# Down-projection of the gated feed-forward layers: a late third output tile at the opening, and four steps of the second group prepared during the first

## The chip, the cores and the metric

The kernel runs on one core of one Trainium2 chip. The metric is the device time of one launch in microseconds (us). Three launches of the kernel before took 1698.48, 1701.52 and 1703.72 us, so the median is 1701.52 us. One more execution was recorded by the hardware profiler; all rows and times of the trace come from it, in us from the first instruction.

## The reference, cut to what matters

Two layers run on 512 latent tokens and 128 context tokens (640 rows), each a token mixer followed by a gated feed-forward block. The change touches only the last product of that block, which is computed once in each of the two layers:

```python
def conv_ffn(h, w_up, conv_w, conv_b, w_down):
    u = h @ w_up                                   # (640, 1024) @ (1024, 5632)
    up = jnp.pad(u, ((0, 0), (1, 1), (0, 0)))
    u = up[:, :-2] * conv_w[0] + up[:, 1:-1] * conv_w[1] + up[:, 2:] * conv_w[2] + conv_b
    a, gt = jnp.split(u, 2, axis=-1)
    return (jax.nn.silu(a) * gt) @ w_down          # (640, 2816) @ (2816, 1024)
...
    xs = xs + g_fs * rmsnorm(fs, norm_ffn_post[l])
```

## The kernel before, in words

**Up-projection.** `ffn` (L1070) makes the 2816 inner columns in 22 pieces of 128 (p = 0 to 21). Each piece is a set of matrix products on PE, evicted by ACT and DVE, then the width-3 convolution in a PSUM tile `t` (ACT L1191, twice DVE L1193), the SiLU (ACT L1199) and the gate product (DVE L1204, `act`), which is stored to DRAM (`act_0` to `act_21`, L1232, on the SP queue). The convolution of the last piece runs after PE's last product.

**Down-projection.** The 640 rows are five output tiles of 128 rows (t = 0 to 4; t = 4 is the context). A tile needs 1024 columns of float32, which is two PSUM banks (`acc`). There are eight banks, so the tiles come in two groups, (0, 1, 2) and (3, 4) (L1337), and each group runs over the 22 steps k of the inner dimension. `load_dn` (L1079) prepares a step: it loads the 128x1024 weight rows (`wr`, 0.5 MB) and the activation columns of the group (`ain`; 384 wide in the first group, 258 in the second), and splits both into a rounded high part and the rest, since the product is made of three passes (high by high, high by low, low by high; `passes`, L166). The high parts `wh` and `ahi` are ACT casts (L155, L1084). The low part `wl` is a subtraction on DVE for even k and on POOL for odd k (L157), `alo` one on DVE (L1086). `go` (L1340) then issues for one tile and one step two halves of three matmuls.

**What sets the order.** `wr`, `wh` and `wl` rotate in four buffers each (pool `wp`), `ahi` and `alo` in four, `ain` in three (pool `dn`). A step can therefore be split only when PE has done all tiles of the step four before it. PE runs its instructions in the order in which the program writes them. The other queues run in the order in which a scheduler placed them, and each is in order, SP's DMA queue too. The first 18 steps go over all tiles of the group; the last four (`tail`) go tile by tile, so that tile 0 is finished first and its bank pair is freed early. While tile 2 does its last four steps, the loop at L1368 prepares steps 0 to 3 of the second group (`NLD` = 4). At the end of a tile, `Finish` does the norm, the residual and, in layer 0, the transposes of the next layer's input (`turns`): square sums on ACT (L327), products on DVE (L344, L346, L356, L365, L371), small scalars on POOL (L329, L336). In layer 0 the transposes of tile 0 run ahead of the last step of tile 2, those of tiles 1 and 2 after steps 3 and 6 of the second group.

**Banks at the opening.** Six of the eight banks belong to the first group. The two banks of tile 2 lie where the convolution tile `t` was, so the first matmul on tile 2 waits for DVE's last read of `t` (L1204).

Of the kernel before, what the change touches and what calls it, by code (L numbers as in the profile page):

```python
# [9 lines left out]
F32 = mybir.dt.float32  # L10
F32R = mybir.dt.float32r
# [7 lines left out]
P = 128  # L19
D = 1024  # L20
# [31 lines left out]
PSN = 4  # L52
PU0 = 6
HALF = (slice(0, 512), slice(512, D))
NLD = 4
KP = (2, 2, 2, 2, 1)
GORDER = ("p s0 t0 va s1 t1 t2".split(), "s0 vb t0 s1 t1 t2".split())

# [33 lines left out]
def hybrid_step(ctx: ExitStack, tc: tile.TileContext, A, O):  # L92
    nc = tc.nc
# [15 lines left out]
    def f32(t):  # L109
        return t.bitcast(F32)  # L110

    def pool(name, bufs=1, side="left", **k):
        return tc.tile_pool(name=name, bufs=bufs, side=side, reuse_waits="tile", **k)

    cst = ctx.enter_context(pool("cst"))
    wp = ctx.enter_context(pool("wp", 4))
# [32 lines left out]

    def wsplit(src, a, b, low=None, own=None, pin=False):  # L150
        q = own or wp
        raw = q.tile([P, a, b], F32, tag="wr", name="wr")
        nc.sync.dma_start(raw, src)
        hi = q.tile([P, a, b], F32R, tag="wh", name="wh")
        i = nc.scalar.copy(hi, raw)  # L155
        lo = q.tile([P, a, b], F32R, tag="wl", name="wl")
        j = (low or nc.vector).tensor_sub(lo, raw, f32(hi))  # L157
        if pin:
            tc.keep_in_program_order(i)
            tc.keep_in_program_order(j)  # L160
        return hi, lo

    def rows(w, r0, nr, c0, ncol):
        return w[r0 * P : (r0 + nr) * P, c0 : c0 + ncol].rearrange("(k p) n -> p k n", p=P)

    def passes(acc, st, w, first, last):  # L166
        for n, (x, y) in enumerate(((st[0], w[0]), (st[0], w[1]), (st[1], w[0]))):
            mm(acc, x, y, start=first and n == 0, stop=last and n == 2)
# [279 lines left out]
    with ExitStack() as s:  # L448
# [57 lines left out]
        def mod_load(i):  # L506
            out = []
            for j in range(4):
                src = rows(A["ada_w"][0], 4 * (j % 2), 4, D - D * (j // 2) + 256 * i, 256)
                how = ADA0[4 * i + j]  # L510
                if how == "r":
                    raw = sp.tile([P, 4, 256], F32, tag="wf", name="wf", bufs=6)
                    nc.sync.dma_start(raw, src)
                    out.append((raw,))
                else:
                    out.append(wsplit(src, 4, 256, nc.gpsimd if how == "p" else None))
            return out
# [41 lines left out]
        def wv_load(i):  # L559
            wv[i] = wsplit(rows(wqkv, 4 * i, 4, 2048, 256), 4, 256, nc.gpsimd)  # L560
# [109 lines left out]
    class Mix:  # L670
# [6 lines left out]
        def weights(self, half, u, low=None):  # L677
            self.ws[half, u] = wsplit(rows(self.w, 2 * u, 2, 512 * half, 512), 2, 512, low, pin=True)
# [35 lines left out]
    with l_na:  # L714
# [268 lines left out]
        for h in range(H):  # L983
# [6 lines left out]
            for i, step in enumerate(order):  # L990
# [15 lines left out]
                if pr and step == "p0":  # L1006
                    sides = []
                    for hh in range(4 * g, 4 * g + 4):
                        qs, kh, kl = qk_of[hh // 2]
                        b = hh % 2  # L1010
# [52 lines left out]
    late = m0.second(fin)  # L1063
# [6 lines left out]
    def ffn(l, hT, hT_close, xold, xnew, nxt, todo, late, late_close, side, back, after=None):  # L1070

        s = ExitStack()
        actd = [dr.tile([P, GAP], F32, name=f"act_{l}_{k}") for k in range(FC)]
        dn = s.enter_context(pool("dn", 4, side))
        cw = cws[l]
        w_up, w_dn = A["ffn_w_up"][l], A["ffn_w_down"][l]
        HB = ((0, 384), (384, GAP))

        def load_dn(k, c0, c1):  # L1079
            w2 = wsplit(rows(w_dn, k, 1, 0, D), 1, D, nc.gpsimd if k % 2 else None)  # L1080
            ain = dn.tile([P, 384], F32, tag="ain", name="ain", bufs=3)
            nc.sync.dma_start(ain[:, 0 : c1 - c0], actd[k][:, c0:c1])
            hi = dn.tile([P, 384], F32R, tag="ahi", name="ahi")
            nc.scalar.copy(hi[:, 0 : c1 - c0], ain[:, 0 : c1 - c0])  # L1084
            lo = dn.tile([P, 384], F32R, tag="alo", name="alo")
            nc.vector.tensor_sub(lo[:, 0 : c1 - c0], ain[:, 0 : c1 - c0], f32(hi[:, 0 : c1 - c0]))  # L1086
            return w2, hi, lo

        lds = deque()
# [7 lines left out]
        with ExitStack() as s2:  # L1097
# [201 lines left out]
            for p in range(PLAIN, FC):  # L1299
                nx = p + 1 if p + 1 < FC else None  # L1300
                for m, q in ((6, p), (5, p), (1, nx), (7, p), (2, nx), (3, p), (4, p)):
                    if q is None:
                        continue
                    evict(m, q, product(m, q))
                    if m == 5:
                        if nx:
                            block_sums(nx)
                        else:
                            lds.append(load_dn(len(lds), *HB[0]))
                    elif m == 7:  # L1310
                        store()
                        if nx:
                            sum_parts(0, nx, nc.gpsimd)
                    elif m == 2:
                        sum_parts(1, nx, nc.gpsimd)
                        if nx + 1 < FC:
                            value(nx + 1, nc.gpsimd)
                    elif m == 3:
                        if not nx:
                            lds.append(load_dn(len(lds), *HB[0]))  # L1320
                        elif nx + 1 < FC:
                            corner(nx + 1)
                    if ada:
                        next(ada, None)
# [8 lines left out]
        xmp = ExitStack()  # L1333
        xmpool = xmp.enter_context(pool("xm", 2, back))
        fin = Finish(l, 5, xold, xnew, nxt, hTn, xmpool, 5, back)
        tail, late = 4, []
        for grp, (c0, c1) in (((0, 1, 2), HB[0]), ((3, 4), HB[1])):  # L1337
            acc = {t: [bk.get("acc") for _ in range(2)] for t in grp}

            def go(t, k, w2, hi, lo, qs=(0, 1)):  # L1340
                c = (t * P if t < 4 else NS + 1) - c0
                for q in qs:
                    passes(acc[t][q], (hi[:, c : c + P], lo[:, c : c + P]),
                           tuple(x[:, 0, 512 * q : 512 * q + 512] for x in w2), k == 0, k == FC - 1)

            for k in range(FC - tail):
                if len(lds) <= k:
                    lds.append(load_dn(k, c0, c1))
                for t in grp:
                    go(t, k, *lds[k])  # L1350
                if nxt and late and k in (3, 6):
                    late.pop(0)()
            for k in range(FC - tail, FC):
                lds.append(load_dn(k, c0, c1))
            prev, lds = lds, deque()
            for t in grp:
                fin.ahead(t)
                if t == 4 and not nxt:
                    for q in range(2):
                        for i in range(tail):  # L1360
                            go(t, FC - tail + i, *prev[FC - tail + i], qs=(q,))
                    fin.end(t, acc[t][0], acc[t][1], fin.stat(acc[t][0]))
                    continue
                for i in range(tail):
                    if nxt and t == 2 and i == tail - 1:
                        late.pop(0)()
                    go(t, FC - tail + i, *prev[FC - tail + i])
                    if t == 2 and i < NLD:  # L1368
                        lds.append(load_dn(i, *HB[1]))
                    if t == 4 and after:  # L1370
                        after(i)
                late.append(fin.end(t, acc[t][0], acc[t][1], fin.stat(acc[t][0])))
# [6 lines left out]
    def gqa_w(c0, u, low=None):  # L1379
        return wsplit(rows(wqkv, 2 * u, 2, c0, 512), 2, 512, low)  # L1380

    wkv = []
    hT, hp2, late, xmp = ffn(
        0, hT, hp1.close, lambda t: xres[0][t], lambda t: xres[1][t], (1, 1, 0, NS),
        ((0, 5), (1, 1), (1, 0), (1, 2), (1, 4), (1, 3)), late, xmp.close, "right", "left",
        lambda u: wkv.append(gqa_w(1024, u)),
    )
# [209 lines left out]
    for hq in range(2):  # L1597
        for n, t in enumerate(((4, 0, 1, 2, 3), (0, 1, 2, 3, 4))[hq]):
# [3 lines left out]
            i = 5 * hq + n  # L1602
# [141 lines left out]
    late = m1.second(fin)  # L1744
# [3 lines left out]
    def y_out(t):  # L1748
        return O["y_sample"][0, t * P : (t + 1) * P, :] if t < 4 else O["y_prompt"][0]

    _, _, _, xmp = ffn(
        1, hT, r_h3.close, lambda t: xres[2][t], y_out, None, ((1, 5),), late, xmp.close, "left", "right"
    )
# [70 lines left out]
```

## Time and profile before

| what | value |
|---|---|
| median of three launches | 1701.52 us (1698.48 to 1703.72) |
| profiled execution, its own time | 1699.22 us |
| its span, first to last instruction | 1697.4 us |
| mean granted TensorE clock | 0.974 |
| layer 0, down-projection (first to last `acc` matmul) | 755.9 to 929.9 us |
| layer 1, down-projection | 1531.5 to 1690.7 us |

A row of the timeline gives the start and the duration of one instruction (or of xN merged ones), the engine, the line, the operation and `out<-in`. Square brackets give the idle time of that engine just before, and what ended it. A matmul's end is modelled, so the pitch from start to start says how fast PE goes.

### The profile page before, as it was taken

The page shows a single profiled execution, that of the slowest core. Times are in us where ns is not written, and L with a number is a line of the kernel's source. Part 1 is how long each engine was busy: PE and PEld are TensorE (multiplying, and loading weights), DVE is VectorE, ACT ScalarE, POOL GpSimd, SP SyncE. Part 2 cuts the span into 40 slices and gives each one's busy share as a digit, 9 for nine tenths or more (in the row PEclk, how much of TensorE's full clock was granted, in tenths as well). Part 3 has the DMA queues.
Part 4 walks back from the last instruction along what each step waited for, and adds up shares of the span by engine and source line. Part 5 has one row for each costly group of instructions (what it writes and reads, how often), then busy time and mean ns, then how long its engine had stood idle before and what let it go on. Part 6 is the DMA issues. An engine that isn't in the chain of part 4 may idle for free.

```text
span 1697.4 us, 26300 instructions
## 1 busy us (share of the span) xinstructions
PE 1589.7 (94%) x9709; PEld 1376.1 (81%) x9709; DVE 1039.7 (61%) x1725; ACT 903.6 (53%) x1721; POOL 751.7 (44%) x651
## 2 busy tenths in 40 slices
PE   6899998999999899989979888999998999998998
PEld 3788897977988788988868666777887999997876
DVE  4444454557875555672375776775696788784264
ACT  5466657655554444553355444664555665663353
POOL 3544545444245354442344345442424555652253
PEclk9999999989999999999989998999999999999999
DMA  9544544116376576347557410001636333336574
GB/s 269 150 112 121 141 127 118 32 63 224 113 235 203 189 218 185 121 153 236 161 187 232 133 38 13 2 1 63 211 112 188 115 120 98 117 117 212 174 238 170
DMA packets 193220, 242.43 MB, mean 143 GB/s; under 512 B 11108, under 2 KB 149572, under 8 KB 193092
## 3 DMA queue, kind: packets, MB, share of 16 engines
q1 hardware_dynamic: 182232, 233.13, 43.7%
q10 hardware_dynamic: 10860, 7.62, 2.3%
q8 instruction: 76, 1.25, 0.3%
q14 instruction: 52, 0.43, 0.1%
HBM read 214.38 MB, written 26.34 MB: 142 GB/s over the span
## 4 chain that ended last, share of the span: by engine, by line
PE 58%; DVE 13%; DMA 8%; POOL 7%; ACT 6%; issue 6%; ACTq 1%; SPq 0%; POOLq 0%; DVEq 0%
PE acc L104 17%; PE ux L104 10%; PE y L104 5%; PE uz L104 4%; PE po L104 3%; PE s L104 3%; DMA wr<-in_ada_w 3%; PE tp L107 3%; PE qk L104 3%; PE uy L104 3%; PE vp L104 3%; DMA wr<-in_na_w_qkv 2%; POOL wl L1117 2%; DVE t L1193 2%; PE ada L104 2%
## 5 line engine op out<-in xcount | busy, mean ns | idle before, releaser
L157 POOL TENSOR_TENSOR wl<-wr,wh 128x1024 fp32r<-128x1024 f32 x80 | 196.3, 2457 | 279.6 <-ACT wh L155 274.9
L1117 POOL TENSOR_TENSOR wl<-wr,wh 128x1024 fp32r<-128x1024 f32 x80 | 194.7, 2451 | 68.7 <-ACT wh L1116 59.3
L104 PE MATMUL ux<-B,wh 128*128 128x322 f32 x832 | 201.9, 313 | 1.9 <-DVE B L210 1.8
L1193 DVE SCALAR_TENSOR_TENSOR t<-C,cw,t 128x644 f32<-128x644 f32 x176 | 156.6, 890 | 55.8 <-ACT t L1191 54.9
L104 PE MATMUL acc<-wh,alo 128*128 128x512 f32 x440 | 175.5, 399 | 10.7 <-DVE alo L1086 10.7
L104 PE MATMUL acc<-wh,ahi 128*128 128x512 f32 x440 | 175.6, 399 | 9.5 <-DVE act L1204 9.5
L155 ACT CAST wh<-wr 128x1024 fp32r<-128x1024 f32 x148 | 153.5, 1047 | 45.0 <-DMA wr<-in_na_w_qkv 17.5
L104 PE MATMUL acc<-wl,ahi 128*128 128x512 f32 x440 | 174.7, 397 | 0.0
L104 PE MATMUL uz<-B,wh 128*128 128x322 f32 x640 | 158.4, 315 | 0.0
L104 PEld LDWEIGHTS ux<-B,wh 128*128 128x128 f32 x832 | 143.6, 189 | 9.6 <-issue 3.3
L1086 DVE TENSOR_TENSOR alo<-ain,ahi 128x384 fp32r<-128x384 f32 (+1 forms) x88 | 55.1, 631 | 141.8 <-ACT ahi L1084 141.8
L104 PE MATMUL ux<-B,wl 128*128 128x322 f32 x416 | 129.2, 311 | 0.0
L1084 ACT CAST ahi<-ain 128x384 fp32r<-128x384 f32 (+1 forms) x88 | 40.5, 462 | 166.3 <-PE acc L104 139.8
L104 PE MATMUL qk<-hT,wh 128*128 128x384 f32 (+1 forms) x512 | 126.6, 320 | 0.4 <-DVE qs L799 0.4
L104 PEld LDWEIGHTS uz<-B,wh 128*128 128x128 f32 x640 | 111.6, 190 | 6.6 <-issue 3.7
L1117 POOL TENSOR_TENSOR vl<-wr,vh 128x1024 fp32r<-128x1024 f32 x38 | 96.5, 2540 | 34.2 <-ACT vh L1116 34.2
L104 PEld LDWEIGHTS acc<-wh,alo 128*128 128x128 f32 x440 | 84.4, 192 | 30.4 <-DVE alo L1086 11.9
L1116 ACT CAST wh<-wr 128x1024 fp32r<-128x1024 f32 x88 | 89.5, 1049 | 35.0 <-DVE wr L1140 33.6
L104 PEld LDWEIGHTS acc<-wh,ahi 128*128 128x128 f32 x440 | 84.6, 192 | 28.4 <-issue 10.2
L1191 ACT ACTIVATE t<-C,cw 128x644 f32<-128x644 f32 x88 | 78.7, 894 | 50.7 <-DVE C L1221 47.4
L157 DVE TENSOR_TENSOR wl<-wr,wh 128x1024 fp32r<-128x1024 f32 x68 | 91.1, 1353 | 21.5 <-ACT wh L155 21.0
L104 PE MATMUL uz<-B,wl 128*128 128x322 f32 x320 | 100.0, 313 | 0.5 <-POOL wl L1117 0.4
(264 smaller groups left out, 4193.8 us busy)
## 6 DMA issues: line engine op xcount, KB each, us to landing
wr<-in_ada_w SPq DMA_DIRECT2D x88, 512.0 KB
wr<-in_ffn_w_up SPq DMA_DIRECT2D x88, 512.0 KB
wr<-in_ffn_w_down SPq DMA_DIRECT2D x88, 512.0 KB
act<-act SPq DMA_DIRECT2D x44, 321.0 KB
wr<-in_na_w_qkv SPq DMA_DIRECT2D x24, 512.0 KB
mod<-modrow SPq DMA_DIRECT2D x20, 512.0 KB
ain<-act SPq DMA_DIRECT2D x44, 192.0 KB
xres<-xo SPq DMA_DIRECT2D x15, 512.0 KB
```

What stands on the lines that cost most here:

```text
L104: pe(nc.tensor.matmul(*a, **k))
L107: pe(nc.tensor.transpose(*a, **k))
L155: i = nc.scalar.copy(hi, raw)
L157: j = (low or nc.vector).tensor_sub(lo, raw, f32(hi))
L1084: nc.scalar.copy(hi[:, 0 : c1 - c0], ain[:, 0 : c1 - c0])
L1086: nc.vector.tensor_sub(lo[:, 0 : c1 - c0], ain[:, 0 : c1 - c0], f32(hi[:, 0 : c1 - c0]))
L1116: nc.scalar.copy(hl[0], src)
L1117: low.tensor_sub(hl[1], src, f32(hl[0]))
L1191: nc.scalar.activation(t, taps(0), AF.Identity, bias=cw[:, 3, n : n + 1], scale=cw[:, 1, n : n + 1])
L1193: nc.vector.scalar_tensor_tensor(t, taps(d), cw[:, w, n : n + 1], t, op0=ALU.mult, op1=ALU.add)
```

## The change: what it does

- **Opening.** In the first group, steps 0, 1 and 2 (`DLEAD` = 3) are done for tiles 0 and 1 only. After step 2, tile 2 does steps 0, 1 and 2 in one go, and from step 3 on all three tiles run together as before.
- **Preloads.** After steps 8, 10, 12 and 14 of the first group (`DPRE`), `load_dn` is called for steps 0 to 3 of the second group, into a pool of their own (`dn2`, four buffers each of `wh`, `wl`, `ahi`, `alo`, three of `ain`). Their raw weights still come through the four `wr` buffers of `wp`.
- **Tail.** During the last four steps of tile 2 the loop now prepares steps 4 to 7 of the second group instead of 0 to 3, in the buffers of `wp` and `dn`.

The number of matmuls, casts, subtractions and loads is the same. The last line of the file and many others move by one to three lines; L104 of before is L105 after, L155 is L156, L1084 is L1086.

```diff
-NLD = 4
+DLEAD = 3
+DPRE = (8, 10, 12, 14)
...
     def wsplit(src, a, b, low=None, own=None, pin=False):
         q = own or wp
-        raw = q.tile([P, a, b], F32, tag="wr", name="wr")
+        raw = wp.tile([P, a, b], F32, tag="wr", name="wr")
         nc.sync.dma_start(raw, src)
         hi = q.tile([P, a, b], F32R, tag="wh", name="wh")
...
-        def load_dn(k, c0, c1):
-            w2 = wsplit(rows(w_dn, k, 1, 0, D), 1, D, nc.gpsimd if k % 2 else None)
-            ain = dn.tile([P, 384], F32, tag="ain", name="ain", bufs=3)
+        def load_dn(k, c0, c1, own=None):
+            w2 = wsplit(rows(w_dn, k, 1, 0, D), 1, D, nc.gpsimd if k % 2 else None, own)
+            p = own or dn
+            ain = p.tile([P, 384], F32, tag="ain", name="ain", bufs=3)
             nc.sync.dma_start(ain[:, 0 : c1 - c0], actd[k][:, c0:c1])
-            hi = dn.tile([P, 384], F32R, tag="ahi", name="ahi")
+            hi = p.tile([P, 384], F32R, tag="ahi", name="ahi")
             nc.scalar.copy(hi[:, 0 : c1 - c0], ain[:, 0 : c1 - c0])
-            lo = dn.tile([P, 384], F32R, tag="alo", name="alo")
+            lo = p.tile([P, 384], F32R, tag="alo", name="alo")
...
-        tail, late = 4, []
+        tail, late, pre = 4, [], deque()
+        dn2 = s.enter_context(pool("dn2", 4, side))
...
                 for t in grp:
-                    go(t, k, *lds[k])
+                    if t != 2 or k >= DLEAD:
+                        go(t, k, *lds[k])
+                if t == 2 and k == DLEAD - 1:
+                    for j in range(DLEAD):
+                        go(2, j, *lds[j])
+                if t == 2 and k in DPRE:
+                    pre.append(load_dn(len(pre), *HB[1], dn2))
...
-            prev, lds = lds, deque()
+            prev, lds, pre = lds, pre, deque()
...
-                    if t == 2 and i < NLD:
-                        lds.append(load_dn(i, *HB[1]))
+                    if t == 2:
+                        lds.append(load_dn(len(lds), *HB[1]))
```

The instruction order shows three places, all in layer 0.

PE at the opening of the down-projection, before: `wh_8191` and `wh_8236` are the weights of steps 0 and 1, `acc_8294` is the second half of tile 1, `acc_8295` and `acc_8296` are tile 2, `acc_8291` is the first half of tile 0.

```order
L104 MATMUL acc_8294<-wh_8191,ahi_8197 128x512
L104 MATMUL acc_8294<-wl_8193,ahi_8197 128x512
L104 MATMUL acc_8294<-wh_8191,alo_8199 128x512
L104 MATMUL acc_8295<-wh_8191,ahi_8197 128x512
L104 MATMUL acc_8295<-wl_8193,ahi_8197 128x512
L104 MATMUL acc_8295<-wh_8191,alo_8199 128x512
L104 MATMUL acc_8296<-wh_8191,ahi_8197 128x512
L104 MATMUL acc_8296<-wl_8193,ahi_8197 128x512
L104 MATMUL acc_8296<-wh_8191,alo_8199 128x512
L104 MATMUL acc_8291<-wh_8236,ahi_8242 128x512
```

The same engine after the change, 24 matmuls further on: `wh_8326` is step 2, `acc_8297` the second half of tile 1, `acc_8298` and `acc_8299` are tile 2.

```order
L105 MATMUL acc_8297<-wh_8326,ahi_8332 128x512
L105 MATMUL acc_8297<-wl_8328,ahi_8332 128x512
L105 MATMUL acc_8297<-wh_8326,alo_8334 128x512
L105 MATMUL acc_8298<-wh_8191,ahi_8197 128x512
L105 MATMUL acc_8298<-wl_8193,ahi_8197 128x512
L105 MATMUL acc_8298<-wh_8191,alo_8199 128x512
L105 MATMUL acc_8299<-wh_8191,ahi_8197 128x512
L105 MATMUL acc_8299<-wl_8193,ahi_8197 128x512
L105 MATMUL acc_8299<-wh_8191,alo_8199 128x512
L105 MATMUL acc_8298<-wh_8236,ahi_8242 128x512
```

Tile 2's first matmul stood behind 12 `acc` matmuls and now stands behind 36.

ACT from the last convolution of the up-projection on, before (the first cast is that of step 4, since steps 0 to 3 are split during the up-projection):

```order
L1191 ACTIVATE t<-C,cw_83 128x2x322
L1084 CAST ahi<-ain 128x384
L155 CAST wh<-wr 128x1024
L1084 CAST ahi<-ain 128x384
L155 CAST wh<-wr 128x1024
L1084 CAST ahi<-ain 128x384
L155 CAST wh<-wr 128x1024
L1084 CAST ahi<-ain 128x384
L155 CAST wh<-wr 128x1024
```

The same place after the change, where the 258 wide casts and the second of the merged weight casts are those of the second group:

```order
L1193 ACTIVATE t<-C,cw_83 128x2x322
L1086 CAST ahi<-ain 128x258 x2
L1086 CAST ahi<-ain 128x384
L156 CAST wh<-wr 128x1024
L1086 CAST ahi<-ain 128x384
L156 CAST wh<-wr 128x1024
L1086 CAST ahi<-ain 128x384
L156 CAST wh<-wr 128x1024
L1086 CAST ahi<-ain 128x258 x2
L1086 CAST ahi<-ain 128x384
L156 CAST wh<-wr 128x1024 x2
```

The scheduler put the four activation casts of the preloads well ahead of step 8, two of them in front of the cast of step 4.

SP at the end of the first group, before (`act_21` with 384 columns is the last activation load of the first group, 258 columns are the second group's):

```order
L1082 DMA ain<-act_21_4825 128x384
L153 DMA wr<-in_ffn_w_down 128x1024
L1082 DMA ain<-act_0_4804 128x258
L153 DMA wr<-in_ffn_w_down 128x1024
L1082 DMA ain<-act_1_4805 128x258
```

The same place after the change:

```order
L1084 DMA ain<-act_21_4825 128x384
L154 DMA wr<-in_ffn_w_down 128x1024
L1084 DMA ain<-act_4_4808 128x258
L154 DMA wr<-in_ffn_w_down 128x1024
L1084 DMA ain<-act_5_4809 128x258
```

The loads that stood here for steps 0 to 3 are now those for steps 4 to 7.

## The prediction

> **What bounds the kernel now.** I began with the page's busy times and its chain of work that ended last.
>
> ```profile
> PE 1589.7 (94%) x9709; PEld 1376.1 (81%) x9709; DVE 1039.7 (61%) x1725; ACT 903.6 (53%) x1721; POOL 751.7 (44%) x651
> PE 58%; DVE 13%; DMA 8%; POOL 7%; ACT 6%; issue 6%; ACTq 1%; SPq 0%; POOLq 0%; DVEq 0%
> ```
>
> PE is busy 94% of the span, and 58% of the chain is PE. The change neither adds nor removes a matmul, so it can only move the gaps in PE's row. I therefore read PE's timeline through both down-projections and looked for starts that lie further apart than the usual pitch. The opening of layer 0:
>
> ```profile
> 755.93 0.40 PE L104 MATMUL acc<-wh,ahi 128*128 128x512 f32 x1
> ...
> 758.47 0.39 PE L104 MATMUL acc<-wh,alo 128*128 128x512 f32 x1
> 763.57 0.76 PE L104 MATMUL acc<-wh,ahi 128*128 128x512 f32 x1 [4.71 <-DVE act L1204]
> ...
> 769.18 0.40 PE L104 MATMUL acc<-wl,ahi 128*128 128x512 f32 x1
> ```
>
> The first two rows are the first and the twelfth matmul, on tiles 0 and 1: the pitch is 2.54 / 11 = 0.231 us. A step of two tiles (12 matmuls) is then 2.77 us, of three tiles 4.16 us. Tile 2 waits for its banks until DVE's last read, and starts at 763.57. The gap costs 5.10 less a pitch, **4.87**. What follows is slow: 13 matmuls take 769.18 - 763.57 = 5.61 instead of 13 x 0.231 = 3.00, another **2.61**.
>
> The change of groups in layer 0, on PE:
>
> ```profile
> 854.42 0.39 PE L104 MATMUL acc<-wl,ahi 128*128 128x512 f32 x1
> 861.15 0.80 PE L104 MATMUL acc<-wh,alo 128*128 128x512 f32 x1 [6.34 <-DVE alo L1086]
> ...
> 864.70 0.40 PE L104 MATMUL acc<-wl,ahi 128*128 128x512 f32 x1
> ...
> 874.60 0.40 PE L104 MATMUL acc<-wl,ahi 128*128 128x512 f32 x1
> 878.19 0.70 PE L104 MATMUL acc<-wh,alo 128*128 128x512 f32 x1 [3.19 <-DVE alo L1086]
> ...
> 881.67 0.42 PE L104 MATMUL acc<-wl,ahi 128*128 128x512 f32 x1
> ```
>
> The second group's first and fifth steps wait for `alo` (854.42 is the eighth matmul of the first step). The gaps cost 6.73 - 0.23 = **6.50** and 3.59 - 0.23 = **3.36**, the eight slow matmuls after each 3.55 - 1.85 = **1.70** and 3.48 - 1.85 = **1.63**. Why `alo` is late, in the rows of ACT, DVE and POOL:
>
> ```profile
> 849.19 0.41 ACT L1084 CAST ahi<-ain 128x258 fp32r<-128x258 f32 x1 [0.38 <-PE acc L104]
> 865.37 1.05 ACT L155 CAST wh<-wr 128x1024 fp32r<-128x1024 f32 x1 [7.21 <-PE acc L104]
> 847.83 1.41 DVE L371 SCALAR_TENSOR_TENSOR xm<-xm,ro,mod 128x512 f32<-128x512 f32 x2 [0.80 <-POOL ro L336]
> 855.18 5.57 DVE L371 SCALAR_TENSOR_TENSOR xm<-xm,ro,mod 128x512 f32<-128x512 f32 x2 [1.08 <-POOL ro L336]
> 860.68 0.75 DVE L1086 TENSOR_TENSOR alo<-ain,ahi 128x258 fp32r<-128x258 f32 x2
> 874.30 3.50 DVE L371 SCALAR_TENSOR_TENSOR xm<-xm,ro,mod 128x512 f32<-128x512 f32 x2 [3.45 <-POOL ro L336]
> 855.12 5.09 POOL L157 TENSOR_TENSOR wl<-wr,wh 128x1024 fp32r<-128x1024 f32 x2
> ```
>
> The first cast of the second group starts only at 849.19, when PE frees a buffer in tile 2's tail, less than 4 us before PE wants the step. Its `alo` then stands on DVE behind the residual of tile 1 (L371), which takes 5.57 beside two POOL subtractions, against 1.41 when POOL is quiet. The fifth step's cast waits 7.21 for PE to finish the first, and its `alo` stands behind tile 2's L371, which ends at 877.8.
>
> Layer 1, PE again, the opening and the change of groups:
>
> ```profile
> 1531.48 0.39 PE L104 MATMUL acc<-wh,ahi 128*128 128x512 f32 x1
> ...
> 1533.99 0.39 PE L104 MATMUL acc<-wh,alo 128*128 128x512 f32 x1
> 1539.13 0.77 PE L104 MATMUL acc<-wh,ahi 128*128 128x512 f32 x1 [4.75 <-DVE act L1204]
> ...
> 1543.95 0.39 PE L104 MATMUL acc<-wh,alo 128*128 128x512 f32 x1
> ...
> 1628.76 0.39 PE L104 MATMUL acc<-wl,ahi 128*128 128x512 f32 x1
> 1630.28 0.50 PE L104 MATMUL acc<-wh,alo 128*128 128x512 f32 x1 [1.13 <-DVE alo L1086]
> ```
>
> The opening costs 5.14 - 0.23 = **4.91** and, over 11 slow matmuls, 4.82 - 2.54 = **2.28** behind it; the change of groups 1.52 - 0.23 = **1.29**.
>
> **The change part by part.** *Opening.* Tiles 0 and 1 now fill 36 matmuls, 36 x 0.231 = 8.32 us, so PE reaches tile 2 at 755.93 + 8.32 = 764.25, and the banks are free at 763.57: 0.68 to spare. In layer 1 it is 1531.48 + 8.32 = 1539.80 against 1539.13, 0.67 to spare. Steps 1 to 3 are split during the up-projection, so nothing else is asked for earlier than it is there. All four terms go: 4.87 + 2.61 + 4.91 + 2.28 = 14.67. If PE comes earlier than the banks by some tenths, the wait is these tenths; bounds 0 to 0.7, I take 0.
>
> What is late next is step 4: its buffers come free when tile 2 has done step 0, at 764.25 + 6 x 0.231 = 765.6. What a split takes is in the page's groups (mean ns after the busy time), the rest in the rows above: `ahi` 0.41 and `alo` 0.38 us in the narrow form, somewhat more in the wide one.
>
> ```profile
> L157 POOL TENSOR_TENSOR wl<-wr,wh 128x1024 fp32r<-128x1024 f32 x80 | 196.3, 2457 | 279.6 <-ACT wh L155 274.9
> L155 ACT CAST wh<-wr 128x1024 fp32r<-128x1024 f32 x148 | 153.5, 1047 | 45.0 <-DMA wr<-in_na_w_qkv 17.5
> L157 DVE TENSOR_TENSOR wl<-wr,wh 128x1024 fp32r<-128x1024 f32 x68 | 91.1, 1353 | 21.5 <-ACT wh L155 21.0
> ```
>
> Two casts (about 1.6) and the low part (1.35 on DVE, 2.46 on POOL for odd steps) make step 4 ready by 768.6; PE wants it after 18 more matmuls of tile 2 and 18 of step 3, at 772.6. Step 5 is ready about 771.5 and wanted at 776.7. So nothing is charged here.
>
> *Preloads.* Each is a load of 0.5 MB and one of 129 KB, two casts on ACT, `alo` on DVE, and `wl` on DVE or POOL. The first group from 764 on, and a denser stretch (PE, PEld, DVE, ACT, POOL busy, clock, DMA share, GB/s):
>
> ```profile
> 764.00:842.00 78.00, 78.00 (x335) 64.27 (x335) 21.07 (x27) 26.50 (x37) 21.50 (x9) 0.97 0.64 203
> 1625.00:1650.00 25.00, 23.87 (x104) 19.16 (x103) 19.54 (x22) 14.98 (x25) 15.66 (x9) 1.00 0.83 272
> ```
>
> In 78 us DVE is busy 21.1, ACT 26.5, POOL 21.5; the preloads add 2 x 1.35 + 4 x 0.38 = 4.2, 4 x (1.05 + 0.41) = 5.8 and 2 x 2.46 = 4.9. DMA moves 203 GB/s, and 2.6 MB more in a slightly shorter time make about 250, under the 272 of the second row. A split can be done three steps (12 us) ahead of its use, so this work lies beside PE and costs nothing. The cover is gone only if loads are later than that (rival 3). On SP two of the preloads' activation loads are queued ahead of the store of `act_21`. They wait for PE's last up-projection product, which ends about when `acc` begins (755.93), while the store waits for DVE until 763.5; they hold nothing back. On ACT two casts of preloads stand ahead of step 4's, whose buffers come free later than these.
>
> *Change of groups.* Steps 0 to 3 are ready long before. Steps 4 to 7 now get the times that steps 0 to 3 had: `alo` of steps 4 and 5 at 860.68 to 861.4. PE runs on from 854.42 without a gap and wants step 4 after 41 more matmuls and eight transposes (a row of eight takes 0.8 here), at 854.42 + 9.47 + 0.8 = 864.7, 3 us later. The transposes of tile 1, wanted at 863.9, need the L371 that ends at 860.7. Tile 2's are wanted three steps later, at 864.7 + 8.3 = 873.0. Their L371 ends at 877.8 in this trace, but its part of the residual stood behind the cast at 865.37 and a POOL subtraction that are both gone from there; I reckon it done about 871. So layer 0's terms go, 6.50 + 1.70 + 3.36 + 1.63 = 13.19, and layer 1's 1.29. For the new meeting points I charge 1 us, bounds 0 and the 3.4 of the old second gap; nearest to nothing, because both margins are positive.
>
> *Clock.* The four long gaps are each followed by matmuls twice as far apart, the gap of 1.13 by none: 2.61 + 1.70 + 1.63 + 2.28 = 8.22 of the sum is this aftermath. The Trainium skill, "TensorE: Matmul & The Clock Gate", section "What's actually happening", says that the PE clock halves after an idle window of about 3.4 us and comes back after about 3.4 us of work. The traces agree in kind. By the page alone four recoveries would cost an estimated 4 x 1.7 = 6.8 us and the sum would be 1.4 smaller.
>
> *Sum.* 14.67 + 13.19 + 1.29 = 29.15, less 1, is 28.15 us. Layer 0's 20.67 must survive to the end: its successor's loads wait for buffers that PE frees, so they move along. The profiled execution took 1699.22 (span 1697.4 and 1.8 around it), 2.3 below the median of the launches, inside their spread. The sum made against it is 1671.1, against the median 1673.4; I take **1672**.
>
> **The rivals.** *1. A new wait in the second group.* DVE and POOL hold each other up: 5.57 against 1.41 above. If tile 1's or 2's residual, or step 4's `alo`, slips by one or two POOL subtractions (2.46 each), PE waits at a transpose or a step. For it: the margins there are 2 to 3 us. Against it: step 4's rows inherit times that have been measured. Price: about the old second gap with its slow tail, 5.0, at most twice that: 1677 to 1682. The Trainium skill, "SBUF — State Buffer", section "Who interferes with whom", says that a DVE instruction with two SBUF inputs and a GpSimd one that reads SBUF exclude each other for the whole instruction. The rows of L371 agree.
>
> *2. Only one half works.* If tile 2 still came too early, or waited for something else, 14.5 of gain would be left, 1701.5 - 14.5 = 1687; if the preloads gave nothing, 14.67 would be left, also 1687. Against it: both openings end on the same DVE line, and by its rows the new order has 0.67 to spare.
>
> *3. Slower: the four `wr` buffers starve the first group.* In steps 8 to 15, twelve loads instead of eight pass through four buffers in 33.3 us, so one turn of a buffer may take 11.1 us. A turn is the landing, 1.05 on ACT and up to 2.46 on POOL, so the pace holds while a load lands within 7.6 us. One landing can be bounded in layer 1, from SP's and ACT's rows:
>
> ```profile
> 1634.28 0.33 SPq L153 DMA_DIRECT2D wr<-in_ffn_w_down  x1
> 1638.71 1.05 ACT L155 CAST wh<-wr 128x1024 fp32r<-128x1024 f32 x1 [1.70 <-DMA wr<-in_ffn_w_down]
> ```
>
> About 4.4 us, at a DMA share of 0.83, so it should hold. Each us over 7.6 delays the stretch by three turns, and the first 12 us are covered. The kernel becomes slower than before from a landing of about 16 us on ((16.3 - 7.6) x 3 - 12 = 14.1 per layer). At 20 us it loses 25.2 per layer, 50.4 - 28.2 = 22 net: 1724.
>
> *4. The change does nothing.* If other engines, not PE, set the pace after each gap, the gaps would reopen later: 1701. PE's 94% speaks against it.
>
> **How the numbers follow.** Forecast 1672, between 1667 and 1676, chance 0.70; rival 1, 1677 to 1682, 0.17; rival 2, 1687, 0.07; rival 4, 0.03; rival 3, 0.03. The range 1665 to 1682 takes in the forecast with its unknown charge, the 2.6 by which launches spread, and rival 1: 0.87, of which some may fall outside. A measurement of this kernel tells about 0.3%, 5.1 us, from no change: faster 0.94, within 0.3% 0.03, slower 0.03.
>
> **What would show it.** In PE's timeline of the changed kernel: the first matmul on tile 2 right behind 36 others in both layers; no gap over 0.7 us and no doubled pitch in the openings; no wait for `alo` at the change of groups; layer 0's down-projection (755.9 to 929.9 now) about 20 us shorter and layer 1's (1531.5 to 1690.7) about 8.5. ACT's `wh` cast should not wait for a `wr` load in the first group. I am wrong if PE waits at a transpose in the second group (rival 1), if the opening's gap stays (rival 2), or if the first group's steps grow beyond 4.2 us around steps 8 to 15 (rival 3).

## The result and the profile after

The kernel after takes 1670.82 us (median of four launches, 1668.97 to 1672.89), the one before 1700.0 (four launches, 1695.11 to 1703.72). The ratio is 0.983, with a 95% interval of 0.9807 to 0.9853: 29.2 us gone. The forecast was 1672, between 1667 and 1676. The profiled execution took 1669.39, 29.83 less than that of before; its span went from 1697.4 to 1667.6.

From the page after, the engines' busy times and shares:

```profile
PE 1579.6 (95%) x9709; PEld 1371.5 (82%) x9709; DVE 1057.2 (63%) x1725; ACT 902.5 (54%) x1721; POOL 751.7 (45%) x651
```

PE's count is the same. Its busy time fell by 10.1 us, all of it in the `acc` matmuls (525.8 to 515.7), since fewer of them run at half rate; the rest of the 29.8 is waiting that is gone.

The opening of layer 0 after, PE's timeline (the first `acc` matmul, then the last on tile 1 and the first on tile 2), and of layer 1:

```profile
755.35 0.40 PE L105 MATMUL acc<-wh,ahi 128*128 128x512 f32 x1
...
763.33 0.39 PE L105 MATMUL acc<-wh,alo 128*128 128x512 f32 x1
763.55 0.39 PE L105 MATMUL acc<-wh,ahi 128*128 128x512 f32 x1
...
1510.35 0.40 PE L105 MATMUL acc<-wh,ahi 128*128 128x512 f32 x1
...
1518.29 0.39 PE L105 MATMUL acc<-wh,alo 128*128 128x512 f32 x1
1518.52 0.39 PE L105 MATMUL acc<-wh,ahi 128*128 128x512 f32 x1
```

Tile 2 follows 36 matmuls (8.20 and 8.17 us) at the usual pitch. DVE's last reads of `t` in the same trace:

```profile
762.02 0.83 DVE L1206 TENSOR_TENSOR act<-t,sl 128x644 f32<-128x644 f32 x1
...
1517.05 0.83 DVE L1206 TENSOR_TENSOR act<-t,sl 128x644 f32<-128x644 f32 x1
```

They end at 762.85 and 1517.88, which is 0.70 and 0.64 before PE starts on tile 2. In the kernel before, PE started 0.15 after the same read had ended (763.42 and 763.57), so the real spare time is about 0.55 and 0.49.

The change of groups in layer 0, PE's timeline around the transposes of tile 1 and tile 2, which stand where the second group's steps 4 and 7 begin:

```profile
856.90 0.39 PE L105 MATMUL acc<-wh,alo 128*128 128x512 f32 x1
857.13 1.04 PE L108 MATMUL tr<-ident,xm 128*128 128x128 f32 x8
857.92 0.48 PE L105 MATMUL acc<-wh,ahi 128*128 128x512 f32 x1
...
866.34 1.03 PE L108 MATMUL tr<-ident,xm 128*128 128x128 f32 x8
867.13 0.48 PE L105 MATMUL acc<-wh,ahi 128*128 128x512 f32 x1
```

DVE there:

```profile
847.04 5.70 DVE L372 SCALAR_TENSOR_TENSOR xm<-xm,ro,mod 128x512 f32<-128x512 f32 x2 [1.08 <-POOL ro L337]
852.66 0.75 DVE L1088 TENSOR_TENSOR alo<-ain,ahi 128x258 fp32r<-128x258 f32 x2
...
861.22 1.42 DVE L372 SCALAR_TENSOR_TENSOR xm<-xm,ro,mod 128x512 f32<-128x512 f32 x2 [1.08 <-POOL ro L337]
```

Tile 1's residual is as slow as before (5.70 against 5.57), and `alo` of steps 4 and 5 still stands behind it, until 853.4. But PE wants it at 858.5 only, because it has steps 0 to 3 to do. The residual is no shorter; PE no longer waits for it. Tile 2's residual is now quick (1.42 against 3.50) and ends at 862.6, 3.7 ahead of its transposes.

Over both down-projections PE has no gap over 0.7 us and no doubled pitch. From the first to the last `acc` matmul, layer 0 takes 153.17 us (173.98 before), layer 1 150.48 (159.17): 20.81 + 8.69 = **29.50**, all of the gain but 0.3.

### The profile page after: what moved, and what is told of

Read it like the earlier page. It is cut to its first block, busy times and chain, and to the rows that moved or that the text cites. A ratio compares the mean times of both kernels' runs of the same rounds, so it can differ in the third digit from the quotient of the medians.

```text
span 1667.6 us, 26282 instructions
## 1 busy us (share of the span) xinstructions
PE 1579.6 (95%) x9709; PEld 1371.5 (82%) x9709; DVE 1057.2 (63%) x1725; ACT 902.5 (54%) x1721; POOL 751.7 (45%) x651
## 4 chain that ended last, share of the span: by engine, by line
PE 47%; DVE 10%; POOL 6%; DMA 4%; issue 4%; ACT 3%; ACTq 0%; SPq 0%; POOLq 0%; DVEq 0%
PE acc L105 18%; PE ux L105 9%; PE uz L105 5%; PE y L105 3%; PE uy L105 3%; POOL wl L1119 3%; DMA wr<-in_ada_w 3%; PE po L105 2%; PE s L105 2%; PE tp L108 2%; DVE t L1195 1%; DVE al L1119 1%; POOL vl L1119 1%; PE ada L105 1%; POOL rh L1437 1%
## 5 line engine op out<-in xcount | busy, mean ns | idle before, releaser
L105 PE MATMUL ux<-B,wh 128*128 128x322 f32 x832 | 201.9, 314 | 1.8 <-DVE B L211 1.7
L156 ACT CAST wh<-wr 128x1024 fp32r<-128x1024 f32 x148 | 153.3, 1047 | 59.6 <-DMA wr<-in_ffn_w_down 28.2
L105 PE MATMUL acc<-wh,alo 128*128 128x512 f32 x440 | 172.0, 391 | 0.0
L105 PE MATMUL acc<-wh,ahi 128*128 128x512 f32 x440 | 171.9, 391 | 0.0
L105 PE MATMUL acc<-wl,ahi 128*128 128x512 f32 x440 | 171.8, 390 | 0.0
L105 PE MATMUL uz<-B,wh 128*128 128x322 f32 x640 | 158.5, 316 | 0.0
L105 PEld LDWEIGHTS ux<-B,wh 128*128 128x128 f32 x832 | 143.8, 189 | 9.5 <-issue 3.7
L1088 DVE TENSOR_TENSOR alo<-ain,ahi 128x384 fp32r<-128x384 f32 (+1 forms) x88 | 74.4, 856 | 89.7 <-ACT ahi L1086 89.3
L105 PE MATMUL ux<-B,wl 128*128 128x322 f32 x416 | 129.3, 311 | 0.0
L105 PE MATMUL qk<-hT,wh 128*128 128x384 f32 (+1 forms) x512 | 126.1, 319 | 0.5 <-DVE qs L800 0.4
L105 PEld LDWEIGHTS uz<-B,wh 128*128 128x128 f32 x640 | 111.9, 190 | 6.6 <-issue 4.1
L1086 ACT CAST ahi<-ain 128x384 fp32r<-128x384 f32 (+1 forms) x88 | 40.1, 460 | 118.9 <-PE acc L105 88.7
L105 PE MATMUL uz<-B,wl 128*128 128x322 f32 x320 | 100.2, 313 | 0.6 <-POOL wl L1119 0.4
L105 PEld LDWEIGHTS acc<-wl,ahi 128*128 128x128 f32 x440 | 82.6, 188 | 17.9
L105 PEld LDWEIGHTS acc<-wh,alo 128*128 128x128 f32 x440 | 82.6, 188 | 17.8
```

The costliest lines, as they stand in the source:

```text
L105: pe(nc.tensor.matmul(*a, **k))
```

## The experiments

All ratios are taken against runs of the kernel before on the same chip (medians 1699.29 for e1 to e4, 1698.88 for e5 and e6, 1696.26 for e7 and e8). A stretch is the time from the first to the last `acc` matmul of a layer in the profiled execution. "Slow" counts the pitches over 0.39 us behind a gap (0.43 is the full half rate; a single one of 0.34 right behind a gap is only the restart).

| kernel | median us | ratio, 95% interval | stretch L0, L1 | PE gaps over 0.6 in L0 (slow after) | in L1 |
|---|---|---|---|---|---|
| before | 1700.0 | | 173.98, 159.17 | 4.87 (12), 6.50 (8), 3.36 (8) | 4.91 (11), 1.29 (0) |
| after | 1670.82 | 0.9807 to 0.9853 | 153.17, 150.48 | none | none |
| e1_opening_only | 1681.46 | 0.9875 to 0.9923 | 165.41, 151.89 | 6.51 (12), 2.96 (0) | 1.29 (0) |
| e2_preloads_only | 1683.53 | 0.9884 to 0.9944 | 160.81, 158.28 | 4.87 (13) | 4.93 (13) |
| e3_lead2 | 1671.25 | 0.9815 to 0.9876 | 155.47, 152.54 | 2.16 (0) | 1.94 (0) |
| e4_two_preloads | 1674.82 | 0.9807 to 0.9881 | 155.90, 150.52 | 1.08 (0), 1.40 (0) | none |
| e5_dense | 1670.45 | 0.9818 to 0.9851 | 153.18, 150.49 | none | none |
| e6_before_dve_low | 1697.54 | 0.9972 to 1.0004 | 170.73, 156.98 | 4.89 (12), 2.35 (7), 4.28 (7) | 4.93 (7) |
| e7_burst | 1671.41 | 0.9819 to 0.9876 | 153.18, 150.52 | none | none |
| e8_lead4 | 1671.28 | 0.9829 to 0.9883 | 153.18, 151.22 | none | 0.61 (0) |

The launches of one kernel spread over some 4 to 14 us; the stretches without gaps agree within 0.05. The spread comes from outside: the first `acc` matmul of layer 0 falls between 753.6 and 760.4 in these traces, and from the end of L0's stretch to the start of L1's pass 597.1 to 602.2. So e3 to e5, e7 and e8 are judged by the stretches; by their times none can be told from the kernel after.

**The opening alone.** The four preloads are taken out, so that the tail prepares steps 0 to 3 of the second group, as before:

```diff
-DPRE = (8, 10, 12, 14)
+DPRE = ()
...
-        dn2 = s.enter_context(pool("dn2", 4, side))
...
-                    pre.append(load_dn(len(pre), *HB[1], dn2))
+                    pre.append(None)
```

> Only the opening is kept (tile 2 joins after three steps); steps 0 to 3 of the second group are prepared in tile 2's tail as before. Theory (each half removes its own gaps and the doubled pitch behind them, and they add): the openings' 14.67 us go, the change of groups keeps its 14.5, so about 1700.0 - 14.7 = 1685 us; layer 0's down-projection 174.0 - 7.5 = 166.5 us with gaps of about 6.5 and 3.4 at its change of groups, layer 1's 159.2 - 7.2 = 152.0. Rival (the halves depend on each other, because the time won at the opening is only lent until the next wait on the split of the second group): the gaps at the change of groups grow by what the opening won, 1695 us or more.

It took 1681.46 against 1699.29. PE at the change of groups of layer 0:

```profile
844.69 0.39 PE L105 MATMUL acc<-wl,ahi 128*128 128x512 f32 x1
851.43 0.80 PE L105 MATMUL acc<-wh,alo 128*128 128x512 f32 x1 [6.35 <-DVE alo L1088]
...
865.79 0.40 PE L105 MATMUL acc<-wl,ahi 128*128 128x512 f32 x1
868.98 0.50 PE L105 MATMUL acc<-wh,alo 128*128 128x512 f32 x1 [2.79 <-DVE alo L1088]
```

The openings' gaps are gone and stay gone, the two gaps behind `alo` are where they were (6.74 - 0.23 = 6.51 and 3.19 - 0.23 = 2.96). The stretches are 8.57 and 7.28 shorter, against 7.48 and 7.19 for the openings' terms; the 1.1 more in layer 0 comes from the second gap and the clock: the second gap is 0.40 shorter and has no slow matmul behind it instead of eight (1.63), the first has twelve instead of eight (0.8 more).

**The preloads alone.**

```diff
-DLEAD = 3
+DLEAD = 0
```

> Only the preloads are kept; tile 2 runs in every step from the first, as before. Theory: both openings keep gaps of 4.9 us and the doubled pitch behind them, the change of groups loses its gaps, so about 1700.0 - 14.5 = 1685.5 us; layer 0's down-projection 174.0 - 13.2 = 160.8 us, layer 1's 159.2 - 1.3 = 157.9. Rival (steps 4 to 7 meet the same jam as steps 0 to 3 did once the first group is not shortened): a gap of 2 to 6 us appears in layer 0's second group, 1690 us or more.

It took 1683.53 against 1699.29. The openings, layers 0 and 1:

```profile
757.41 0.39 PE L105 MATMUL acc<-wh,alo 128*128 128x512 f32 x1
762.51 0.77 PE L105 MATMUL acc<-wh,ahi 128*128 128x512 f32 x1 [4.71 <-DVE act L1206]
...
1518.33 0.39 PE L105 MATMUL acc<-wh,alo 128*128 128x512 f32 x1
1523.49 0.77 PE L105 MATMUL acc<-wh,ahi 128*128 128x512 f32 x1 [4.77 <-DVE act L1206]
```

Both are as before, and no gap is left at the changes of groups. The stretches are 13.17 and 0.89 shorter, against 13.19 and 1.29 for these terms (layer 1's opening had two slow matmuls more in this trace, 2.68 against 2.28). The two halves make 15.85 + 14.06 = 29.9, both together 29.50: they add, and neither needs the other. The medians (17.8 and 15.8 us below their kernel before) are too spread to test this, with intervals of 13.1 to 21.2 and 9.5 to 19.7.

**Two steps of lead instead of three.**

```diff
-DLEAD = 3
+DLEAD = 2
```

> Tile 2 joins after two steps instead of three, the preloads stay. PE then reaches tile 2 after 24 matmuls, 5.54 us, while the banks come 7.64 us after the first matmul: a gap of 2.1 us in each layer. Theory A (the doubled pitch comes only after a gap above a threshold that lies between the 1.1 us gap that had none and the 3.2 us gap that had it): 4.2 us lost in all or up to 3.4 more if 2.1 is above the threshold in both layers; without it 1675 us and no pitch of 0.43 behind the gap. Theory B (the slow stretch grows with the gap, about half of it): 4.2 + 2 = 6.3 us lost, 1677 us, with a few matmuls at 0.43. The Trainium skill, TensorE: Matmul & The Clock Gate, section What's actually happening, puts the threshold at an idle window of about 3.4 us; by it there is no slow pitch here.

PE at tile 2's start, layers 0 and 1:

```profile
760.66 0.39 PE L105 MATMUL acc<-wh,alo 128*128 128x512 f32 x1
763.05 0.47 PE L105 MATMUL acc<-wh,ahi 128*128 128x512 f32 x1 [2.01 <-DVE act L1206]
...
1513.19 0.39 PE L105 MATMUL acc<-wh,alo 128*128 128x512 f32 x1
1515.36 0.47 PE L105 MATMUL acc<-wh,ahi 128*128 128x512 f32 x1 [1.78 <-DVE act L1206]
```

The wait for DVE is back, at 2.16 and 1.94: what 24 matmuls (5.5 us) leave of the 7.65 and 7.39 until the banks are free. The stretches are 2.30 and 2.06 longer than after, 4.4 together, and the doubled pitch stays away. That is theory A with 2.1 below its threshold, and not theory B; but e6 below has the doubled pitch behind a gap of 2.35 and e1 none behind 2.96, so no threshold on the gap alone holds. Three steps is the smallest lead that covers the banks. The time, 1671.25 (1669.11 to 1678.03), does not resolve the 4.4.

**Four steps of lead.**

```diff
-DLEAD = 3
+DLEAD = 4
```

> DLEAD = 4: tile 2 comes in after 48 matmuls instead of 36, nothing else. Theory (the opening only needs to be longer than the 7.64 us until the banks are free; 36 matmuls are 8.32 us): nothing is left to win, PE has no gap over 0.7 us at tile 2's start, and the two stretches stay at 153.2 and 150.5 us. The buffers of step 4 come free 12 x 0.231 = 2.8 us later than with 3 steps, at about 768.4 us, and step 4 is ready about 3 us later, 771.4, against 772.6 when PE wants it; odd steps are 1.1 us later. So a gap up to 1 us may stand at step 4 or 5. Time 1669 to 1674. Rival (buffers, not banks, set the pace at the opening: the split of step 4 and 5 is late once tile 2 starts later): a gap of 2 us or more at step 4 or 5 in both layers, with slow matmuls, 1675 to 1682.

No gap in layer 0, and one of 0.61 in layer 1, at step 13 and not at step 4 or 5, where it was looked for. PE, then POOL and ACT just before:

```profile
1559.63 0.39 PE L105 MATMUL acc<-wh,ahi 128*128 128x512 f32 x1
1560.47 0.50 PE L105 MATMUL acc<-wl,ahi 128*128 128x512 f32 x1 [0.45 <-POOL wl L158]
...
1555.33 7.75 POOL L158 TENSOR_TENSOR wl<-wr,wh 128x1024 fp32r<-128x1024 f32 x3 [5.58 <-ACT wh L156]
...
1554.20 2.00 ACT L156 CAST wh<-wr 128x1024 fp32r<-128x1024 f32 x2 [5.24 <-DMA wr<-in_ffn_w_down]
```

PE waits there for the second of three low parts that stand in a row on POOL (it ends at 1560.41), and they stand in a row after ACT had waited 5.24 for a weight load and then cast several weights close together. So there is nothing left to win beyond three steps; the rival's gaps of 2 us at steps 4 and 5 did not come, but with four steps the cover of the loads was used up at this one place. The cover can be read from the rows as the time from the end of a step's `alo` on DVE to the first matmul that uses it, for steps 5 to 17 of the first group. It is 11.6 us for every step of the kernel before, at least 4.9 (layer 0) and 4.6 (layer 1) after the change, and at least 5.4 and 1.75 here. Why the load came that late was not followed.

**Two preloads instead of four.**

```diff
-DPRE = (8, 10, 12, 14)
+DPRE = (8, 10)
```

> Only steps 0 and 1 of the second group are preloaded, during steps 8 and 10; the tail prepares steps 2 to 5. Theory (the preloads buy PE time until the split of the tail is through the jam of tile 1's residual, 8.7 us after the first transposes): PE wants step 2 about 6.3 us after the start of these transposes and waits some 2.4 us in layer 0, perhaps 0 to 3 more at step 6, and not at all in layer 1: 1673 to 1677 us. Rival (each preload is worth a fourth of the gaps): half of 14.5 comes back, 1678 us, with a gap in layer 1 too.

PE in layer 0's second group:

```profile
856.87 0.40 PE L105 MATMUL acc<-wl,ahi 128*128 128x512 f32 x1
858.18 0.51 PE L105 MATMUL acc<-wh,alo 128*128 128x512 f32 x1 [0.92 <-DVE alo L1088]
...
869.81 0.40 PE L105 MATMUL acc<-wh,ahi 128*128 128x512 f32 x1
871.44 0.50 PE L105 MATMUL acc<-wl,ahi 128*128 128x512 f32 x1 [1.23 <-DVE wl L158]
```

Two steps give PE two times 12 matmuls less cover, and two small gaps come back, 1.08 at step 2 and 1.40 at step 6; layer 1 needs no more than two. The places are those expected, and the first gap is less than half of the 2.4 that was reckoned. So the third and fourth preload are worth 2.7 us by the stretches.

**The preloads denser, and in one burst.** First behind four steps in a row, then all four behind step 14, which asks most of the four `wr` buffers:

```diff
-DPRE = (8, 10, 12, 14)
+DPRE = (8, 9, 10, 11)
```

> The four preloads come after steps 8, 9, 10 and 11 instead of every second step, so that eight weight loads instead of six pass through the four raw buffers within four steps. Theory (loads and splits are three steps ahead, and a load lands in about 4.4 us): no gap on PE, the same time as the changed kernel, 1671 us within 2. Rival (the four raw buffers starve the first group: a turn may take only 16.6 / 2 = 8.3 us here, of which 3.5 are splits, so that loads must land in 4.8 us): ACT's weight casts wait for loads in steps 10 to 15 and PE waits some us before step 16, 1675 us or more.

```diff
-DPRE = (8, 10, 12, 14)
+DPRE = (14,)
...
-                    pre.append(load_dn(len(pre), *HB[1], dn2))
+                    for j in range(4):
+                        pre.append(load_dn(j, *HB[1], dn2))
```

> All four preloads are written behind step 14 of the first group, in a row, instead of behind steps 8, 10, 12 and 14; the same work. The question is how far the first group's loads are ahead of their use. After the change ACT's weight cast waited for loads 13.3 us in all in layer 0's first group, though PE never waited. Theory (the cover is about three steps, 12 us, and four more loads take one turn of the four wr buffers, about 4.4 + 1.05 + 2.46 = 8 us): ACT waits longer in one place, PE does not wait or under 1 us per layer, and the time is that of the kernel after, 1668 to 1674. Rival (the cover is only about one load, and ACT's waits of up to 4.6 us were already its end): PE waits 3 us or more for alo or wl of steps 15 to 17 in each layer, with slow matmuls behind it, and the time is 1676 to 1686.

Both have the stretches of the kernel after, within 0.04. ACT's waits for weight loads in 755 to 850 us (us in total, times, longest us), of the kernel after:

```profile
ACT wh L156 <- DMA wr<-in_ffn_w_down: 13.3, 5, 4.6
```

of the dense one:

```profile
ACT wh L156 <- DMA wr<-in_ffn_w_down: 10.8, 5, 3.4
```

and of the burst:

```profile
ACT wh L156 <- DMA wr<-in_ffn_w_down: 8.7, 6, 2.9
```

ACT does wait for loads, which it never did in this part before, but PE does not wait in any of the three. The burst was to make the longest wait longer, and made it shorter, 2.9 against 4.6 (3.6 against 2.6 for an activation load), so its expectation was right on PE and wrong on ACT. Neither order of the preloads used up the cover of the first group's loads; only the fourth step of lead did, above.

**The low parts of two steps on DVE, in the kernel before.** The two POOL subtractions beside tile 1's residual (second group's steps 1 and 3) go to DVE:

```diff
-            w2 = wsplit(rows(w_dn, k, 1, 0, D), 1, D, nc.gpsimd if k % 2 else None)
+            w2 = wsplit(rows(w_dn, k, 1, 0, D), 1, D, nc.gpsimd if k % 2 and (c0 == 0 or k > 3) else None)
```

> The kernel before, with one edit: the low parts of steps 1 and 3 of the second group are subtracted on DVE instead of POOL. Theory (the first step's activation was late because tile 1's residual on DVE was held by POOL's two subtractions): the two instructions of that residual take about 1.4 us instead of 5.57, the first step's gap shrinks from 6.5 to about 2.4 us with little or no doubled pitch behind it, so about 5 to 6 us less in layer 0 from the first gap; DVE has 2.7 us more work, so the second gap may stay: 1693 to 1696 us. Rival (the buffers came free too late anyway, the residual is slow for another reason): the residual still takes 5 us or more, the gap stays at 6 us, 1700 us.

DVE in layer 0:

```profile
853.08 1.41 DVE L371 SCALAR_TENSOR_TENSOR xm<-xm,ro,mod 128x512 f32<-128x512 f32 x2 [1.08 <-POOL ro L336]
...
868.95 3.48 DVE L371 SCALAR_TENSOR_TENSOR xm<-xm,ro,mod 128x512 f32<-128x512 f32 x2 [3.44 <-POOL ro L336]
```

and PE:

```profile
852.30 0.39 PE L104 MATMUL acc<-wl,ahi 128*128 128x512 f32 x1
854.88 0.50 PE L104 MATMUL acc<-wh,alo 128*128 128x512 f32 x1 [2.19 <-DVE alo L1086]
...
868.31 0.40 PE L104 MATMUL acc<-wl,ahi 128*128 128x512 f32 x1
872.82 0.80 PE L104 MATMUL acc<-wh,alo 128*128 128x512 f32 x1 [4.12 <-DVE alo L1086]
```

With POOL quiet tile 1's residual takes 1.41 instead of 5.57 (4.16 less), and the gap behind it is 2.35 instead of 6.50 (4.15 less). So the hold between DVE and POOL made nearly two thirds of the old first gap. Tile 2's residual still runs beside a POOL subtraction (3.48), and its gap is 4.28 instead of 3.36. The stretches are 3.25 and 2.19 shorter. In layer 1 the gap of 1.29 at the change of groups is gone, and the opening happened to have seven slow matmuls behind it instead of eleven. The expectation had the residual and the first gap right. It missed that seven slow matmuls would follow that gap and that the second gap would grow, so layer 0 won 3.25 and not 5 to 6. The time, 1697.54, is inconclusive: a ratio of 0.9988 with an interval that takes in 1. The preloads win far more without touching that hold.

## Why the prediction was right, point by point

- **The openings** (14.67). Shown by e1 and e3. The spare time was reckoned at 0.68 and 0.67 and is about 0.55 and 0.49, positive as it had to be; a step less brings back the gap that its 12 matmuls covered.
- **The change of groups** (14.48). Shown by e2, and e4 gives part of it back. The reckoning of the margins in layer 0 was close. To compare, 8.06 is added to the times after (755.93 - 755.35 = 0.58 and the 7.48 of the opening). The `alo` of steps 4 and 5 are then done at 861.5 (reckoned 861.4), tile 1's transposes come at 865.2 (863.9), tile 2's residual ends at 870.7 (871) and its transposes come at 874.4 (873.0). All margins are positive and 1 to 2 us wider than thought.
- **The charge of 1 us for new meeting points** was not needed: it is 0. The sum without it, 29.15, stands against 29.50 measured in the stretches. Some 0.23 of the last 0.35 is matmuls behind the gaps that the forecast did not count: single pitches between 0.23 and 0.43 that end a slow stretch, and the restart behind the gap of 1.13.
- **The clock's aftermath** (8.22 of the sum) went with the gaps, but the reason given, long gaps are followed by slow matmuls and one of 1.13 by none, is too simple: how long a gap is does not settle it (last section).
- **The rivals.** A new wait in the second group did not come. A half that does not work was excluded by e1 and e2. The gain survived to the end of the launch: outside the two stretches the profiled executions differ by 0.3. That they differ by so little is luck, since the time outside the stretches lies between 1359.3 and 1367.6 in the ten traces. By the same spread it is luck that the median came within 1.2 of the forecast.
- **What failed is the step on the cover of the first group's loads.** I wrote that the preloads' work "lies beside PE and costs nothing" with 4.2 us more on DVE, a landing of about 4.4, and that ACT's cast should not wait for a `wr` load. The result holds, the working does not. Equal stretches of the first group (7.5 us apart, as the opening moved it), of before, in the columns that the prediction names:

```profile
771.50:832.50 61.00, 61.00 (x271) 50.52 (x270) 16.95 (x22) 22.03 (x30) 18.88 (x8) 1.00 0.64 204
```

and of after:

```profile
764.00:825.00 61.00, 61.00 (x271) 50.52 (x270) 30.91 (x28) 27.95 (x39) 24.41 (x10) 1.00 0.84 283
```

PE does the same 271 rows in both. ACT (+5.9) and POOL (+5.5) are near the 5.8 and 4.9 reckoned. DVE gained 14.0 instead of 4.2, and DMA moves 283 GB/s, not 250 and not within the 272 taken as a bound. DVE's groups in the same windows, before and after, say where its time went:

```profile
L1086 DVE TENSOR_TENSOR alo<-ain,ahi 128x384 fp32r<-128x384 f32 x15 | 8.4, 558 | 41.4 <-ACT ahi L1084 41.4
```

```profile
L1088 DVE TENSOR_TENSOR alo<-ain,ahi 128x384 fp32r<-128x384 f32 x16 | 18.8, 1181 | 18.7 <-ACT ahi L1086 18.4
```

One `alo` takes 1181 ns on average instead of 558. Before, ACT split one step at a time in PE's rhythm, so DVE's short subtraction and POOL's long one kept apart. After, ACT waits for a load and then splits two steps at once:

```profile
790.81 2.00 ACT L156 CAST wh<-wr 128x1024 fp32r<-128x1024 f32 x2 [4.64 <-DMA wr<-in_ffn_w_down]
792.72 0.92 ACT L1086 CAST ahi<-ain 128x384 fp32r<-128x384 f32 x2
...
793.25 3.01 DVE L1088 TENSOR_TENSOR alo<-ain,ahi 128x384 fp32r<-128x384 f32 x2
...
792.89 2.48 POOL L158 TENSOR_TENSOR wl<-wr,wh 128x1024 fp32r<-128x1024 f32 x1 [5.59 <-ACT wh L156]
```

and `alo` falls beside a POOL `wl`. The 16 single rows of `alo` agree: five take 2.45 to 2.74, and for over 2 us of each POOL is at a `wl`; one during which a `wl` begins takes 0.56; the ten that no `wl` overlaps take 0.54 to 0.56, and so do all 15 of before, which no `wl` overlaps either. That makes 10.4 of the 14.0, and what is left is near the 4.2 reckoned. One of the five, at 768, stands in the same place in e1, without any preload (2.60), so that one comes with the late third tile. No run takes these POOL subtractions away; that they are what holds `alo`, as in e6, rests on the rows. The hold is paid out of DVE's idle time, and the late loads out of the cover: the `alo` of a step, done 11.6 us before its use in the kernel before (12 were reckoned), is done as little as 4.6 us before it.

## What to carry to other kernels

When one engine is busy 94% of the span, a list of its gaps with what ended each is already a good forecast: four kinds of gap, priced from start to start, gave 29.15 of 29.50 us. To take away a wait it is enough to put other ready work of the same engine in front of it, and the amount can be counted in advance (8.3 us of matmuls against 7.6 us until the banks are free); a fourth step brings nothing and one step less brings back the difference. Work that is said to cost nothing because an engine is idle should be priced beside what will run at the same time, since on DVE the sum of durations measured alone was too small by a factor of three here.

## What the runs showed of the hardware

- **The slow matmuls after a gap do not follow from its length alone.** A gap of 2.35 (e6) was followed by seven, one of 3.36 (before) by eight; one of 2.96 (e1) and those of 2.16 and 1.94 (e3) by none. Gaps of 4.28 to 6.51 always had 7 to 13. The Trainium skill, "TensorE: Matmul & The Clock Gate", section "What's actually happening", says that the activity window is free-running, so that the place of the change varies. The scatter agrees with that; that a gap of 2.35, shorter than the page's window of about 3.4, is enough does not follow from it. For the gaps between 2 and 3.4 us seen here the price was the length, or the length and 1.6 to 1.7 us more.
- **What the slow matmuls did follow.** In each trace the granted clock changes only at points that lie whole multiples of 3.41 us apart. So the time can be cut into steps of 3.41 us, and PE's idle time in each read from its rows. Two such steps from the gap of 2.35 (e6), then two from one of 2.16 (e3); the columns are those named in the prediction:

```profile
852.35:855.77 3.42, 1.23 (x6) 0.76 (x5) 2.69 (x4) 3.42 (x8) 0.81 (x3) 1.00 0.68 254
855.77:859.18 3.41, 3.41 (x10) 2.67 (x9) 3.41 (x7) 0.64 (x3) 2.39 (x3) 0.50 0.75 213
...
759.49:762.90 3.41, 1.56 (x7) 0.94 (x6) 2.61 (x3) 0.70 (x1) 0.00 (x0) 1.00 0.58 208
762.90:766.31 3.41, 3.25 (x14) 2.73 (x15) 0.89 (x3) 1.82 (x4) 0.00 (x0) 1.00 0.74 185
```

With 2.19 idle in the step the clock is 0.50 in the next, with 1.85 it stays at 1.00. Over both down-projections of all ten traces, every step at full clock with 2.19 or more of idle PE was followed by half clock, and none with 1.85 or less. Half clock ended after a step with 0.30 or less idle and went on after one with 0.99 or more. It lasted one step (7 or 8 slow matmuls) or two (8 to 13). So the price of a gap depends on its length and on where it falls: in e1's second gap PE was idle for 2.79, but with 0.98 in one step and 1.81 in the next.

- **DVE beside POOL.** The same pair of L371 took 1.41 alone, 3.48 or 3.50 beside one POOL subtraction and 5.57 or 5.70 beside two: each POOL subtraction (2.35 to 2.84 in these places) adds some 2.1 us.
